# Two quarter-size column groups multiplied by seven products of halves, with their weights summed by accumulating loads and the engines' chains linked half a step apart

## The chip, the cores and the metric

The kernel runs on one core of a Trainium2 chip. Its engines are called here PE (matrix products; PEld is its weight load), DVE (element-wise), ACT (activation functions and casts), POOL and SP (SP issues transfers, POOL can too). The metric is the device time of one launch in microseconds (us). Before the change it is 914.13 us, the median of three runs from 913.93 to 915.59 us.

## The reference, cut to what matters

```python
xn = rms_norm(x, norm_pre_w)                      # x: 256 tokens x 2048
z = xn @ w_in                                     # 2048 x 13312
u, g_lru, q, k, v, g_attn, m_lru, m_attn = split(z)
u = centred_depthwise_conv(u, conv_w, conv_b)     # width 4
h = rg_lru(u, forward) + rg_lru(u, reverse)
y_a = h * silu(g_lru)
y_b = windowed_gqa(rope(q), rope(k), v, sink) * silu(g_attn)
merged = sigmoid(m_lru) * (y_a @ w_proj_a) + sigmoid(m_attn) * (y_b @ w_proj_b)
out = x + rms_norm(merged @ w_out)
```

All is float32. Two of the matrices are touched by the change: the recurrent merge gate (`m_lru`, 2048 columns of `w_in`) and projection pa (`w_proj_a`, 2048 x 2048).

## The kernel before, in words

The weights pass through the core once, in 152 loads of 1 MB. Each load is one *step*. A "quad" step holds 512 rows by 512 columns of a weight matrix, and four quads make one chunk of 512 output columns; a "blk" step holds all 2048 rows of 128 columns. Steps run in the order of `load_plan` (L53): input u, merge gate 0, v, then blocks of the gates gl and ga and of u, with merge-gate chunks 1, 2 and 3 set between (`BETWEEN`), then k, four times (q, pa), four chunks of ma, four of pb, four of o.

Products are made to near float32 accuracy from two parts of each operand: the high part is a cast to float32r and the low part is the rest. A 512-column product takes three matmuls (high by high, high by low, low by high; `mm3`, L155).

Each step is cut into two *half steps*, numbered `hs`. In half step `hs` the program issues, in this order, the loads that have come due (`fetch(i + 3)`, three `raw` buffers), then all work registered for it (`at`, `soon`), then the split of the weights for half step `hs + 4` (`split`, L146: ACT casts `wh`, L115; DVE subtracts to `wl`, L116; five buffers of each), then the matmuls of `hs` itself. The engines each follow this order on their own, so PE can only be held up by a `wh` or `wl` that is late, by a PSUM bank that isn't free, or by an activation part that is late.

In the recurrent stage `lru_pair` (L410) spreads the work of one pair of blocks over 20 half steps: convolution on DVE (`conv`), the gate matmuls `gate..` in four PSUM banks of tag `bg` (which has four), sigmoids, tanh, exp and square root on ACT, products and scans on DVE. Pairs start `PACE` half steps apart. Attention heads start four half steps apart.

SBUF work tiles of 4 KB a partition come from a pool `units` of 32.

Of the kernel before, what the change touches and what calls it, by code (L numbers as in the profile page):

```python
# [20 lines left out]
P = 128  # L21
D = 2048
S = 256
# [5 lines left out]
UNITS = 32  # L29
# [3 lines left out]
LRU0 = 13  # L33
BETWEEN = {1: 1, 3: 2, 5: 3}
XN = 15
PACE = (20,) + (16,) * 6 + (12,) * 2
HEAD0 = 5
FIRST = 8
# [14 lines left out]
def load_plan():  # L53

    plan = []

    def quad(m, c):
        plan.extend(("quad", m, c, i) for i in range(4))

    def pair(m, c, n):  # L60
        plan.extend(("blk", m, c + (n + i) * P, 0) for i in range(2))

    quad("w_in", U0)
    quad("w_in", ML0)
    quad("w_in", V0)
    for i in range(8):
        pair("w_in", GL0, 2 * i)
        pair("w_in", GA0, 2 * i)
        if i < 6:
            pair("w_in", U0, 2 * i + 4)  # L70
        if i in BETWEEN:
            quad("w_in", ML0 + BETWEEN[i] * 512)
    quad("w_in", K0)
    for c in range(4):
        quad("w_in", Q0 + c * 512)
        quad("w_proj_a", c * 512)
    for c in range(4):
        quad("w_in", MA0 + c * 512)
    for c in range(4):
        quad("w_proj_b", c * 512)  # L80
    for c in range(4):
        quad("w_out", c * 512)
    return plan


def body(ctx, tc, x, xT, wall, wlru, pvec, npost, ident_d, mask_d, rope_d, out):
    nc = tc.nc
    const = ctx.enter_context(tc.tile_pool(name="const", bufs=1))
    units = ctx.enter_context(tc.tile_pool(name="units", bufs=UNITS))
    ring = ctx.enter_context(tc.tile_pool(name="ring", bufs=3))  # L90
# [30 lines left out]
    plan = load_plan()  # L121
# [16 lines left out]
    raws, parts = {}, {}  # L138

    def fetch(i):  # L140
        if i >= len(plan) or i in raws:
            return
        raws[i] = ring.tile([P, 2048], F32, tag="raw", name=f"raw{i}", bufs=3)
        nc.sync.dma_start(raws[i], wall[i])

    def split(q, c=0, w=1024, cast=nc.scalar.copy):  # L146
        i, h = q // 2, q % 2
        if i >= len(plan):
            return
# [10 lines left out]
    def add_pair(name, act, done):  # L160
# [23 lines left out]
        for j in range(2):  # L184
            steps.append(("blk", lambda h, wh, wl, j=j: half(j, h, wh, wl)))

    def total(dst, ps):
        t = half_unit("total", "lo", F32, 1)
        nc.scalar.copy(t, ps[:, :, 1])
        nc.vector.tensor_tensor(dst, ps[:, :, 0], t, ALU.add)  # L190

    def add_rows(name, act, done, spare=False, last=False):
# [33 lines left out]
        for g in range(4):  # L226
            steps.append(("quad", lambda h, wh, wl, g=g: half(g, h, wh, wl)))
# [134 lines left out]
    for g in range(4):  # L362
        steps.append(("quad", lambda h, wh, wl, g=g: u_quad(g, h, wh, wl)))
# [3 lines left out]
    def upad_tile(n):  # L367
        t = small.tile([P, 2, S + 3], F32, tag="upad", name=f"upad{n}", bufs=2)
        nc.gpsimd.memset(t[:, :, 0:2], 0.0)
        nc.gpsimd.memset(t[:, :, S + 2:S + 3], 0.0)  # L370
        upads[n] = t
        return t
# [4 lines left out]
    def evac_quad(n):  # L377
        scaled(upad_tile(n)[:, :, 2:2 + S], ups[n // 2][:, :, 0])
# [31 lines left out]
    def lru_pair(n, b):  # L410
# [7 lines left out]
        def weights():  # L418
            v["wh"] = unit(f"lwh{n}", F32R, (P, 1024))
            v["wl"] = unit(f"lwl{n}", F32R, (P, 1024))  # L420
            parts_of(v["wh"], v["wl"], v.pop("raw"))

        def conv(j):
            if j == 0:
                v["u"] = half_unit(f"uu{n}", "uu")
            up = upads[n]
# [3 lines left out]
            nc.vector.tensor_scalar(u, up[:, j, 0:S], cw[:, 0:1], cb, ALU.mult, ALU.add)  # L430
            for tap in range(1, 4):
                nc.vector.scalar_tensor_tensor(u, up[:, j, tap:tap + S], cw[:, tap:tap + 1], u, ALU.mult, ALU.add)  # L432
# [3 lines left out]
        def u_parts():  # L436
            v["uh"] = half_unit(f"uh{n}", "ph", F32R, 1)
            v["ul"] = half_unit(f"ul{n}", "pl", F32R, 1)
            parts_of(v["uh"], v["ul"], v["u"])
# [46 lines left out]
        def y_parts():  # L486
            q = n // 2
            ya[q] = pair_unit(f"ya{q}")
            parts_of(ya[q][:, :, 0], ya[q][:, :, 1], sgl[n // 4][:, n % 4:n % 4 + 2])

# [12 lines left out]
        at(b + 21 + G, y_parts)  # L503

    def silu_evac(units_list, n):
        def done(ps):
# [5 lines left out]
            nc.scalar.activation(sg, dst, AF.Sigmoid)  # L512
            soon(lambda: nc.vector.tensor_tensor(dst, dst, sg, ALU.mult))
        return done

    def u_evac(n):
        return lambda ps: total(upad_tile(n)[:, :, 2:2 + S], ps)

    tm, sm, ms = [], [], []

    def gate_evac(units_list, c, scale=1.0):
        def done(t, ps):
            if t == 0:
                units_list.append(unit(f"mg{c}", F32, (P, 2, 512)))
            nc.scalar.activation(units_list[c][:, t], ps, AF.Sigmoid, scale=rtok[:, t:t + 1] if scale is None else scale)
        return done

    add_rows("ml0_", xs, gate_evac(tm, 0, None), True)
# [9 lines left out]
    add_rows("v_", xs, v_evac)  # L538

    b = LRU0  # L540
    for c in range(8):
        add_pair(f"gl{2 * c}", xn, silu_evac(sgl, 2 * c))
        add_pair(f"ga{2 * c}", xn, silu_evac(sga, 2 * c))
        if c < 6:
            add_pair(f"u{2 * c + 4}", xn, u_evac(2 * c + 4))
        if c in BETWEEN:
            add_rows(f"ml{BETWEEN[c]}_", xn, gate_evac(tm, BETWEEN[c]))
# [295 lines left out]
```

## Time and profile before

| | |
|---|---|
| median of three runs | 914.13 us |
| the profiled execution's own time | 914.31 us |
| its span, first to last instruction | 912.5 us |
| PE busy | 903.0 us (99%), 4638 matmul records |
| PEld busy | 772.1 us (85%) |
| DVE busy | 610.6 us (67%), 841 instructions |
| ACT busy | 551.7 us (60%), 775 instructions |
| moved by transfers | 172.18 MB, mean 189 GB/s |
| mean granted TensorE clock | 0.997 |

A matmul's bar in the trace is longer than its share of PE's time, since matmuls overlap: two that follow each other start closer together than one lasts. PE's pace is therefore read from starts, or from the chain of waits, where each piece is cut at the start of the next. For DVE and ACT the mean duration of a group is close to what one instruction takes.

### The profile page before, as it was taken

To read this page: it belongs to the slowest core of one execution; us is meant where nothing else is said; L and a number is where in the kernel's file an instruction comes from. 1 tells how busy PE (TensorE), PEld (TensorE's weight loads), DVE (VectorE), ACT (ScalarE), POOL (GpSimd) and SP (SyncE) were. 2 spreads that over 40 slices of the span, in tenths; PEclk is the share of its full clock that TensorE was granted. 3 is DMA by queue.
4 is the path that set the end of the run, shared out by engine and by line. 5 is a ranking of instruction groups with operands and counts; after the bars stand their busy time and mean duration, and the time that the engine had idled before them with its cause. 6 is when DMAs were issued, how large, how long until landed. Compare 5 with 4: busy or idle time off the path is not lost.

```text
span 912.5 us, 11845 instructions
## 1 busy us (share of the span) xinstructions
PE 903.0 (99%) x4638; PEld 772.1 (85%) x4638; DVE 610.6 (67%) x841; ACT 551.7 (60%) x775; POOL 1.4 (0%) x23
## 2 busy tenths in 40 slices
PE   9999999999999999999999999999999999999996
PEld 8888888888888888888888888888888888888885
DVE  6897877768676868596755666666654655555554
ACT  7969578685969496949445545454554544444451
POOL 0000000000000000000000000000000000000000
PEclk9999999999999999999999999999999999999998
DMA  9744564545564455536654444444444555558532
GB/s 329 261 180 170 194 254 181 208 142 191 199 216 176 184 180 214 181 136 217 218 190 154 173 166 158 151 172 163 161 167 175 204 191 185 185 191 316 185 139 92
DMA packets 27703, 172.18 MB, mean 189 GB/s; under 512 B 3072, under 2 KB 3968, under 8 KB 8576
## 3 DMA queue, kind: packets, MB, share of 16 engines
q1 hardware_dynamic: 26928, 170.27, 51.7%
q10 hardware_dynamic: 720, 1.16, 0.3%
q8 instruction: 36, 0.59, 0.2%
q14 instruction: 19, 0.16, 0.0%
HBM read 169.32 MB, written 2.10 MB: 188 GB/s over the span
## 4 chain that ended last, share of the span: by engine, by line
PE 98%; DMA 1%; DVE 0%; ACT 0%; issue 0%; SPq 0%; DVEq 0%
PE ga L175 6%; PE gl L175 6%; PE u L175 5%; PE o L156 4%; PE o L158 4%; PE o L157 4%; PE ga L177 3%; PE gl L177 3%; PE u L177 3%; PE u_ps L360 2%; PE gate L156 1%; PE gate L158 1%; PE gate L157 1%; PE ma__6163 L156 1%; PE pa__5483 L156 1%; PE ma__5943 L156 1%
## 5 line engine op out<-in xcount | busy, mean ns | idle before, releaser
L116 DVE TENSOR_TENSOR wl<-raw,wh 128x1024 fp32r<-128x1024 f32 (+1 forms) x306 | 370.5, 1215 | 265.0 <-ACT wh L115 264.1
L115 ACT CAST wh<-raw 128x1024 fp32r<-128x1024 f32 (+1 forms) x305 | 315.5, 1045 | 212.1 <-PE o L158 37.0
L175 PE MATMUL gl<-xn,wh 128*128 128x512 f32 x256 | 62.5, 391 | 0.0
L175 PE MATMUL ga<-xn,wh 128*128 128x512 f32 x256 | 62.5, 391 | 0.0
L175 PEld LDWEIGHTS gl<-xn,wh 128*128 128x128 f32 x256 | 46.8, 188 | 9.0
L175 PEld LDWEIGHTS ga<-xn,wh 128*128 128x128 f32 x256 | 46.8, 188 | 9.0
L156 PE MATMUL o<-wh,ms 128*128 128x512 f32 x128 | 49.9, 390 | 0.0
L158 PE MATMUL o<-wh,ms 128*128 128x512 f32 x128 | 49.8, 389 | 0.0
L157 PE MATMUL o<-wl,ms 128*128 128x512 f32 x128 | 49.8, 389 | 0.0
L175 PE MATMUL u<-xn,wh 128*128 128x512 f32 x192 | 46.8, 391 | 0.0
L175 PEld LDWEIGHTS u<-xn,wh 128*128 128x128 f32 x192 | 35.3, 188 | 6.8
L617 ACT ACTIVATE p<-p,nm 128x256 f32<-128x256 f32 x32 | 16.0, 502 | 36.3 <-DVE nm L615 36.3
L177 PEld LDWEIGHTS gl<-xn,wl 128*128 128x128 f32 x256 | 33.0, 191 | 1.3
L177 PEld LDWEIGHTS ga<-xn,wl 128*128 128x128 f32 x256 | 33.0, 191 | 1.3
L177 PE MATMUL ga<-xn,wl 128*128 128x256 f32 x256 | 33.7, 283 | 0.0
L177 PE MATMUL gl<-xn,wl 128*128 128x256 f32 x256 | 33.7, 283 | 0.0
L158 PEld LDWEIGHTS o<-wh,ms 128*128 128x128 f32 x128 | 24.0, 188 | 5.0
L157 PEld LDWEIGHTS o<-wl,ms 128*128 128x128 f32 x128 | 24.0, 188 | 5.0
L156 PEld LDWEIGHTS o<-wh,ms 128*128 128x128 f32 x128 | 24.0, 188 | 4.9
L177 PEld LDWEIGHTS u<-xn,wl 128*128 128x128 f32 x192 | 24.6, 191 | 0.9
L177 PE MATMUL u<-xn,wl 128*128 128x256 f32 x192 | 24.9, 283 | 0.0
L432 DVE SCALAR_TENSOR_TENSOR uu<-upad,pv,uu 128x256 f32<-128x256 f32 x48 | 23.3, 485 | 2.3
(345 smaller groups left out, 2012.7 us busy)
## 6 DMA issues: line engine op xcount, KB each, us to landing
raw<-wall_dram SPq DMA_DIRECT2D x149, 1024.0 KB, 4.8
lraw<-wlru_dram SPq DMA_DIRECT2D x8, 512.0 KB, 5.7
raw<-wall_dram SPq DMA_DIRECT2D x4, 512.0 KB, 7.0
xr<-x_dram SPq DMA_DIRECT2D x4, 512.0 KB, 10.2
raw<-wall_dram SPq DMA_DIRECT2D x4, 256.0 KB, 5.1
xT<-xT_dram SPq DMA_DIRECT2D x4, 256.0 KB, 6.4
np<-npost_dram SPq DMA_DIRECT2D x2, 512.0 KB, 7.7
out_dram<-yw SPq DMA_DIRECT2D x4, 256.0 KB, 2.1
```

What stands on the lines that cost most here:

```text
L115: cast(h, src)
L116: nc.vector.tensor_tensor(l, src, h.bitcast(F32), ALU.subtract)
L156: nc.tensor.matmul(ps, wh, xh, start=start, stop=False)
L157: nc.tensor.matmul(ps, wh, xl, start=False, stop=False)
L158: nc.tensor.matmul(ps, wl, xh, start=False, stop=stop)
L175: nc.tensor.matmul(ps, wh[:, sl], a, start=k == 0, stop=k == KT - 1)
L177: nc.tensor.matmul(ps[:, 1], wl[:, sl], a[:, 0], start=False, stop=False)
L360: nc.tensor.matmul(ups[b // 2][:, b % 2, 0], w[:, sl], a[:, m], start=k == 0 and n == 0, stop=k == KT - 1 and n == 2)
L432: nc.vector.scalar_tensor_tensor(u, up[:, j, tap:tap + S], cw[:, tap:tap + 1], u, ALU.mult, ALU.add)
L617: nc.scalar.activation(p[:, t], p[:, t], AF.Exp, bias=nm[:, t:t + 1], accum_out=dn[:, t:t + 1])
```

## The change

**Seven products.** Merge-gate chunks 1 and 2, and pa's chunks 2 and 3, are no longer multiplied chunk by chunk. Each pair of chunks is a product of a 256 x 2048 by a 2048 x 1024 matrix; both are cut in halves each way (128 tokens, 1024 rows of the weights, 512 columns), and the four quarter results come from seven products (`add_seven`, `SEVEN`) in place of eight. Each product is two *woven* steps, so fourteen steps with half the matmuls of a plain step (12, against 24) stand where eight plain ones stood. `spread` sets one woven step behind every three plain ones in the recurrent stage, and one behind one or two plain ones among pa and pb. The total is 164 steps.

**Sums on the left.** Four of the seven products take differences of quarters of the activations: `sums` makes them on DVE (L600) from the normalised input (`xe`) and from the recurrent branch's output (`ye`), and splits them into high and low parts.

**Sums on the right.** The weights of q5, n7, n6 and q4 are sums of quarters. The tile of the earlier product is kept (pool `chain`, two buffers), and POOL issues a load that adds the next quarter to it (`accum_op=ALU.add`, L870), once both halves of the tile are split. There are 16 such loads of 1 MB. SP issues 145 loads of 1 MB from the loop, against 149 before.

**Putting together.** `after` copies or combines each product on ACT or DVE; two products that share a PSUM bank accumulate in it, so that bank is held from one woven step to the next. Pool `units` has 31 tiles.

**Links half a step apart.** `ahead` issues the cast `wh` for `hs + 4` in `hs`, and `low` the subtraction `wl` in `hs + 1` (before, both in `hs`). `lag_parts` does the same to other splits, `total` and the silu to theirs; heads get a half step between `expo` and `powers`. The recurrent pairs start an even 18 half steps apart (`LRU_PACE`), the heads three. The convolution reads a tile without borders, so POOL's memsets of borders are gone. ma's chunks stand between the q's, and pa comes behind them.

```diff
+CHAIN = 2
-LRU0 = 13
+LRU0 = 14
+LRU_PACE = 18
-PACE = (20,) + (16,) * 6 + (12,) * 2
+HEADS_PACE = 3
+FILL = ((0,), (1,), (), (2, 3))
...
+SEVEN = {
+    "p1": (0, 0, "r"), "p2": (0, 1, None), "q5": (1, 0, "r"), "n3": (1, 1, "q"),
+    "n7": (1, 0, "q"), "n6": (0, 0, "q"), "q4": (0, 1, "q"),
+}
...
+    def lag_parts(h, l, src):
+        nc.scalar.copy(h, src)
+        soon(lambda: nc.vector.tensor_tensor(l, src, h.bitcast(F32), ALU.subtract))
...
     def fetch(i):
-        if i >= len(plan) or i in raws:
+        if i >= len(steps) or i in raws or i in grown:
             return
-        raws[i] = ring.tile([P, 2048], F32, tag="raw", name=f"raw{i}", bufs=3)
-        nc.sync.dma_start(raws[i], wall[i])
+        if i in grow:
+            raws[i] = chain.tile([P, 2048], F32, tag="c", name=f"chain{i}")
+        else:
+            raws[i] = ring.tile([P, 2048], F32, tag="raw", name=f"raw{i}", bufs=3)
+        nc.sync.dma_start(raws[i], wall[rows_of[steps[i][0]]])
...
+    def add_seven(name, m, cols, left, take):
...
+        def half(op, s, h, wh, wl):
+            fresh = op in ("p1", "q5", "n7", "q4")
+            if fresh and s == 0 and h == 0:
+                ps["at"] = bank(f"{name}{op}", (P, 512))
+            d = ps["at"]
+            for j in range(2):
+                k = 4 * s + 2 * h + j
+                a, b = left(op, k)
+                sl = slice(j * 512, (j + 1) * 512)
+                for n, (x, y) in enumerate(((a, wh), (a, wl), (b, wh))):
+                    nc.tensor.matmul(d, x, y[:, sl], start=fresh and k == 0 and n == 0, stop=k == 7 and n == 2, skip_group_check=not fresh)
+            if s == 1 and h == 1:
+                soon(lambda: after(op, d))
...
+            elif op == "n6":
+                w = t["w"] = scrap(3)
+                tt(w, d, t["p1"], ALU.subtract)
+                tt(t["x"], t["x"], w, ALU.add)
+                tt(t["q5"], t["q5"], w, ALU.add)
+                soon(lambda x=t["x"], y=t["q5"]: [take(0, 1, x), take(1, 1, y)])
...
+        def less(d, a, b):
+            e[d] = e[b] if isinstance(b, str) else eight(unit(f"{name}{d}"))
+            for n in range(2):
+                f = [e[o][:, 4 * n:4 * n + 4] if isinstance(o, str) else fm(*o, n) for o in (a, b)]
+                nc.vector.tensor_tensor(e[d][:, 4 * n:4 * n + 4], *f, ALU.subtract)
...
+    for c in range(8):
+        lru_pair(2 * c, LRU0 + LRU_PACE * c)
+    steps += spread(plain, add_seven("ml", "w_in", [ML0 + 512, ML0 + 1024], lefts(xn, xe), lambda t, j, d: gate_take(tm, 1 + j, t, d)), 8, 3)
...
+    steps += spread(plain, add_seven("pa", "w_proj_a", [3 * 512, 2 * 512], lefts(pa, ye), lambda t, j, d: take_pa(3 - j, t, d)), 2, 1.3)
...
+    def low(q):
+        i, h = q // 2, q % 2
+        wh, wl = parts[q]
+        nc.vector.tensor_tensor(wl, raws[i][:, h * 1024:(h + 1) * 1024], wh.bitcast(F32), ALU.subtract)
+        if h == 1 and i in grow:
+            n = grow[i]
+            raws[n] = raws[i]
+            nc.gpsimd.dma_start(raws[n], wall[rows_of[steps[n][0]]], accum_op=ALU.add)
+
+    def ahead(q):
+        if q < 2 * len(steps):
+            i, h = q // 2, q % 2
+            parts[q] = [ring.tile([P, 1024], F32R, tag=f"w{s}", name=f"w{s}{i}_{h}", bufs=5) for s in "hl"]
+            nc.scalar.copy(parts[q][0], raws[i][:, h * 1024:(h + 1) * 1024])
+            soon(lambda: low(q))
```

How instructions stand on three engines shows the places that the prediction speaks of. In the rows, a name carries the step and half that it belongs to: `wl26_1` is the low part for the second half of step 26, `gr2` belongs to the recurrent pair that starts at block 2.

DVE in the recurrent stage, where the scans of pair 2 meet the convolution of pair 4; before:

```order
L430 TENSOR_SCALAR uu4_1531<-upad4_1180,pv_90 128x256
L432 SCALAR_TENSOR_TENSOR uu4_1531<-upad4_1180,pv_90,uu4_1531 128x256 x3
L116 TENSOR_TENSOR wl26_1_1537<-raw26_1462,wh26_1_1536 128x1024
L499 TENSOR_TENSOR gi2_1326<-gi2_1326,th2_1378 128x1024
L430 TENSOR_SCALAR uu4_1531<-upad4_1180,pv_90 128x256
L432 SCALAR_TENSOR_TENSOR uu4_1531<-upad4_1180,pv_90,uu4_1531 128x256 x3
L116 TENSOR_TENSOR wl27_0_1560<-raw27_1506,wh27_0_1559 128x1024
L476 SCALAR_TENSOR_TENSOR gr2_1325<-a2_1407,gi2_1326 128x256
L477 SCALAR_TENSOR_TENSOR gr2_1325<-a2_1407,gi2_1326 128x256
L476 SCALAR_TENSOR_TENSOR gr2_1325<-a2_1407,gi2_1326 128x256
L477 SCALAR_TENSOR_TENSOR gr2_1325<-a2_1407,gi2_1326 128x256
L116 TENSOR_TENSOR lwl4_1580<-lraw4_1439,lwh4_1579 128x1024
```

and in the change (`xee4l` is the low part of one of the activation sums):

```order
L467 SCALAR_TENSOR_TENSOR gr2_1298<-a2_1366,gi2_1299 128x256
L468 SCALAR_TENSOR_TENSOR gr2_1298<-a2_1366,gi2_1299 128x256
L467 SCALAR_TENSOR_TENSOR gr2_1298<-a2_1366,gi2_1299 128x256
L468 SCALAR_TENSOR_TENSOR gr2_1298<-a2_1366,gi2_1299 128x256
L420 TENSOR_SCALAR up4_1177<-up4_1177,pv_93 128x256
L423 SCALAR_TENSOR_TENSOR up4_1177<-up4_1177,pv_93 128x254
L423 SCALAR_TENSOR_TENSOR up4_1177<-up4_1177,pv_93 128x255 x2
L866 TENSOR_TENSOR wl26_1_1510<-raw26_1440,wh26_1_1509 128x1024
L420 TENSOR_SCALAR up4_1177<-up4_1177,pv_93 128x256
L423 SCALAR_TENSOR_TENSOR up4_1177<-up4_1177,pv_93 128x254
L423 SCALAR_TENSOR_TENSOR up4_1177<-up4_1177,pv_93 128x255 x2
L113 TENSOR_TENSOR xee4l_1521<-xee1_1172,xee4h_1520 128x1024
```

The four scans and one half of the convolution now stand in one half step, where they stood on two sides of a weight split, and a sum's low part has come between the splits.

PE at the second gate group of pair 4 (`gate4_10` and `gate4_11` are the third and fourth PSUM bank that the pair takes); before, the row in which the fourth bank begins had no wait:

```order
L156 MATMUL gate4_10_1716<-uh4_1601,lwh4_1579 128x256
L157 MATMUL gate4_10_1716<-ul4_1602,lwh4_1579 128x256
L158 MATMUL gate4_10_1716<-uh4_1601,lwl4_1580 128x256
L156 MATMUL gate4_11_1723<-uh4_1601,lwh4_1579 128x256
L157 MATMUL gate4_11_1723<-ul4_1602,lwh4_1579 128x256
```

and in the change:

```order
L152 MATMUL gate4_10_1727<-uh4_1609,lwh4_1582 128x256
L153 MATMUL gate4_10_1727<-ul4_1610,lwh4_1582 128x256
L154 MATMUL gate4_10_1727<-uh4_1609,lwl4_1583 128x256
L152 MATMUL gate4_11_1734<-uh4_1609,lwh4_1582 128x256 [waits Activation_49]
L153 MATMUL gate4_11_1734<-ul4_1610,lwh4_1582 128x256
```

The fourth bank now waits for ACT, whose sigmoids empty the first one. The same wait stands at the pairs 4 to 12; at pair 14 it is one on DVE, and pairs 0 and 2 have none.

POOL's queue; before, it held the memsets of borders:

```order
L369 MEMSET upad4_1180 128x2x2 [waits DVE_49,Pool_49]
L370 MEMSET upad4_1180 128x2
L369 MEMSET upad6_1508 128x2x2 [waits DVE_49,Pool_49]
L370 MEMSET upad6_1508 128x2
L369 MEMSET upad8_2027 128x2x2 [waits DVE_49,Pool_49]
```

and in the change it holds the accumulating loads (here pa's):

```order
L870 DMA chain112_5685<-wall_dram 128x2048 [waits DMAHW2_49,DMASW6_49,DVE_49]
L870 DMA chain114_5831<-wall_dram 128x2048 [waits DMAHW4_49,DMASW7_49,DVE_49]
L870 DMA chain125_6317<-wall_dram 128x2048 [waits DMAHW5_49,DMASW0_49,DVE_49]
L870 DMA chain128_6436<-wall_dram 128x2048 [waits DMAHW0_49,DMASW1_49,DVE_49]
L870 DMA chain125_6317<-wall_dram 128x2048 [waits DMASW2_49,DVE_49]
L870 DMA chain128_6436<-wall_dram 128x2048 [waits DMASW3_49,DVE_49]
L870 DMA chain125_6317<-wall_dram 128x2048 [waits DMASW4_49,DVE_49]
L870 DMA chain128_6436<-wall_dram 128x2048 [waits DMASW5_49,DVE_49]
```

Each waits for DVE's last subtraction from the tile and for the load into it before.

More of the change, by code (lines that the diff above doesn't have):

```diff
@@ L28 @@
 EPS = 1e-6
-UNITS = 32
+UNITS = 31
+CHAIN = 2
 DECAY = 12
@@ L182, in half @@
                 soon(lambda: done(got["ps"]))
-        for j in range(2):
-            steps.append(("blk", lambda h, wh, wl, j=j: half(j, h, wh, wl)))
+        return [(("blk", m, c + (n + j) * P, 0), lambda h, wh, wl, j=j: half(j, h, wh, wl), None) for j in range(2)]
     def total(dst, ps):
@@ L536, in v_evac, with spread @@
         nc.vector.scalar_tensor_tensor(vl, ps, rtok[:, t:t + 1], vh.bitcast(F32), ALU.mult, ALU.subtract)
-    add_rows("v_", xs, v_evac)
-    b = LRU0
+    steps += add_rows("v_", "w_in", V0, xs, v_evac)
+    def spread(plain, woven, start, every):
+        plain, at_ = list(plain), [start + int(n * every) for n in range(len(woven))]
+        for n, i in reversed(list(enumerate(at_))):
+            plain.insert(i, woven[n])
+        assert at_[-1] <= len(plain) - len(woven), (at_, len(plain))
+        return plain
@@ new lines, in add_seven, with scrap, after @@
+    def add_seven(name, m, cols, left, take):
+        ps, t = {}, {}
+        def half(op, s, h, wh, wl):
[11 more added lines that the diff above has]
+                soon(lambda: after(op, d))
+        def scrap(n):
+            if n % 2 == 0:
+                t["two"] = unit(f"{name}t{n}", F32, (P, 2, 512))
+            return t["two"][:, n % 2]
+        def after(op, d):
+            tt = nc.vector.tensor_tensor
+            if op == "p1":
+                t["p1"] = scrap(0)
+                nc.scalar.copy(t["p1"], d)
+            elif op == "p2":
+                take(0, 0, d)
+            elif op == "q5":
+                t["q5"] = scrap(1)
+                nc.scalar.copy(t["q5"], d)
+            elif op == "n3":
+                t["x"] = scrap(2)
+                nc.scalar.copy(t["x"], d)
+            elif op == "n7":
+                tt(t["x"], t["x"], d, ALU.subtract)
+            elif op == "n6":
[4 more added lines that the diff above has]
+                soon(lambda x=t["x"], y=t["q5"]: [take(0, 1, x), take(1, 1, y)])
+            else:
+                tt(t["w"], d, t["w"], ALU.subtract)
+                soon(lambda w=t["w"]: take(1, 0, w))
+                t.clear()
+        out = []
+        for op, (c, r, key) in SEVEN.items():
+            for i in range(2):
+                out.append((("quad", m, cols[c], 2 * r + i), lambda h, wh, wl, op=op, i=i: half(op, i, h, wh, wl), key and (name, key, i)))
+        return out
@@ new lines, in lefts, with left @@
+    def lefts(pairs, e):
+        of = {"p1": (0, 0), "p2": (0, 1), "q4": (1, 1), "q5": "e1", "n3": "e4", "n7": "e3", "n6": "e2"}
+        def left(op, k):
+            o = of[op]
+            if isinstance(o, str):
+                return [a[:, k] for a in e[o]]
+            k += 8 * o[1]
+            return [pairs[k // 2][:, k % 2, m, o[0] * P:(o[0] + 1) * P] for m in range(2)]
+        return left
+    xe, xe_when = sums("xe", xt)
+    xe_when([XE + n for n in (0, 6, 12, 18)])
+    plain = []
@@ new lines, in ms_flip, with ms_part, branch, rows @@
+    def ms_flip(c, held):
+        for q in range(2):
+            held[q] = bank(f"ms_ps{c}{q}")
+            for j in range(2):
+                n = 2 * q + j
+                for t in range(2):
+                    nc.tensor.transpose(held[q][:, j, t * P:(t + 1) * P], sm[c][:, t, n * P:(n + 1) * P], ident)
+    def ms_part(c, q, held):
+        a = pair_unit(f"ms{2 * c + q}")
+        ms[2 * c + q] = a
+        lag_parts(a[:, :, 0], a[:, :, 1], held.pop(q))
+    def branch(name, m, y, take):
+        pairs = {}
+        def rows(q):
+            a = pairs[q] = pair_unit(f"{name}y{q}")
+            lag_parts(a[:, :, 0], a[:, :, 1], y[q // 2][:, q % 2 * 2:q % 2 * 2 + 2])
+        def when(hs):
+            for q in range(8):
+                at(hs + q, lambda q=q: rows(q))
+        def chunk(c):
+            return add_rows(f"{name}{c}_", m, c * 512, pairs, lambda t, d: take(c, t, d))
+        return pairs, when, chunk
@@ L769, in body @@
             if hs >= FIRST:
-                split(hs + 4)
+                ahead(hs + 4)
             half(h, *parts.pop(hs))
```

239 lines of the change are left out of this document (110 added, 129 removed).

## The prediction

> **What bounds the kernel now.** I read the page first: its head, the busy times and the chain that ended last.
>
> ```profile
> span 912.5 us, 11845 instructions
> PE 903.0 (99%) x4638; PEld 772.1 (85%) x4638; DVE 610.6 (67%) x841; ACT 551.7 (60%) x775; POOL 1.4 (0%) x23
> PE 98%; DMA 1%; DVE 0%; ACT 0%; issue 0%; SPq 0%; DVEq 0%
> ```
>
> PE is the bound from end to end: 98% of the chain is PE work. A busy PE isn't yet a PE that can't be held up, so next come the waits of PE alone, which name all that ever held it.
>
> ```profile
> PE spin L240 <- POOL eps L235: 1.0, 1, 1.0
> PE u_ps L360 <- ACT wh L115: 0.8, 2, 0.5
> PE kp L583 <- issue: 0.4, 1, 0.4
> ```
>
> That is 2.2 us in all, most of it at the start. Then the chain in order of time gives PE's pace and the tail. A wide matmul (512 columns) takes 3.65/16 = 0.228 us of PE, a half-width one 1.91/16 = 0.119 us.
>
> ```profile
> 79.40 1.91 PE gl L177 x16
> 81.31 3.65 PE gl L175 x16
> ...
> 905.03 0.24 PE o L158
> 905.27 0.02 issue
> 905.29 0.70 ACT junk L733 x2
> ```
>
> So a plain quad step is 24 x 0.228 = 5.47 us, a blk step 3.65 + 1.91 = 5.56 us. After the last matmul, 912.5 - 905.3 = 7.2 us of tail remain, which the change leaves alone. The time can fall only by PE work that goes away, and rises by whatever starves PE.
>
> How near are the two engines that feed PE? The stretches of the recurrent stage (80 to 440 us) and of q, pa, ma (440 to 760 us), with columns PE, PEld, DVE, ACT, POOL busy, clock, transfer share and GB/s:
>
> ```profile
> 80.00:440.00 360.00, 359.56 (x1995) 314.31 (x1995) 265.96 (x320) 268.97 (x361) 0.68 (x10) 1.00 0.53 191
> 440.00:760.00 320.00, 320.00 (x1553) 268.75 (x1552) 197.50 (x335) 159.25 (x241) 0.00 (x0) 1.00 0.48 172
> ```
>
> DVE and ACT are busy 74% and 75% of the first and 62% and 50% of the second. The recurrent stage is the tight one.
>
> **The change, part by part.**
>
> *PE work removed.* Each pair of chunks was 8 steps of 24 wide matmuls, 192; now it is 14 of 12, 168. Two pairs save 48, which is also the difference between the two listings of PE (3200 wide matmuls, now 3152; the narrower ones are unchanged in number). 48 x 0.228 = 10.9 us, all of it on the chain.
>
> *Splits added.* Fourteen woven steps replace eight, so there are 2 x 6 x 2 = 24 more weight splits. The sums of activations add 8 splits of the same size and 16 half-size subtractions; the rest is copying and combining. Counted on the listings, DVE gets 32 instructions of 1024 elements and 34 of 512 more, ACT 32 and 6.
>
> ```profile
> L116 DVE TENSOR_TENSOR wl<-raw,wh 128x1024 fp32r<-128x1024 f32 x302 | 367.8, 1222 | 263.8 <-ACT wh L115 262.9
> L432 DVE SCALAR_TENSOR_TENSOR uu<-upad,pv,uu 128x256 f32<-128x256 f32 x48 | 23.3, 485 | 2.3
> L476 DVE TENSOR_TENSOR_SCAN gr<-a,gi 128x256 f32<-128x256 f32 x16 | 10.8, 674 | 0.0
> L460 DVE TENSOR_TENSOR gi<-gi,uu 128x512 f32<-128x512 f32 x16 | 10.3, 685 | 0.0
> L430 DVE TENSOR_SCALAR uu<-upad,pv 128x256 f32<-128x256 f32 x16 | 6.4, 402 | 0.0
> L115 ACT CAST wh<-raw 128x1024 fp32r<-128x1024 f32 x302 | 313.6, 1049 | 211.0 <-PE o L158 37.0 <-PE pb__6626 L158 13.5 <-PE pb__6940 L158 13.5
> L189 ACT COPY total<-ga 128x512 f32<-128x512 f32 x8 | 4.6, 573 | 1.8 <-PE ga L175 1.8
> ```
>
> DVE: 32 x 1.222 + 34 x 0.685 = 62 us, to about 673 us, 75% of a span near 902. ACT: 32 x 1.049 + 6 x 0.573 = 37 us, to some 589 us, 65%. Both lie beside PE on average; if nothing hid them, DVE's 62 us would be the price. The question is the densest place.
>
> That place is half steps 48 to 55, where the first rows shown of the change stand: scans of pair 2, convolution of pair 4 and two of the activation sums. Its DVE list holds 11 instructions of 1024 elements, 9 of 512, 4 scans, and a convolution of 2 plus 6: 11 x 1.222 + 9 x 0.685 + 4 x 0.674 + 2 x 0.402 + 6 x 0.485 = 26.0 us. PE takes 2 x 6 x 0.228 (the two half steps of a woven step, 6 wide matmuls each) + 6 x 2.78 (halves of blk steps) = 19.4 us. DVE falls 6.6 us behind. Its lead: `wl` of half step q is now issued in q - 3, so two plain half steps, 5.5 us, may pass before PE needs it (before, three). Back to back, DVE is a little faster than its means:
>
> ```profile
> 310.41 2.35 DVE L116 TENSOR_TENSOR wl<-raw,wh 128x1024 fp32r<-128x1024 f32 x2
> ```
>
> 1.175 us apiece, 4% less, which makes the lag 5.6 us. So PE waits between 0 (DVE enters this place ahead, since it can subtract as soon as the cast is there) and about 1.1 us (it enters with none to spare). The same count before gives at most 24.0 us against 23.7, and PE never waited. Four other groups of eight half steps exceed PE, at 64, 120, 136 (recurrent) and 224 (pa): 21.3, 22.7 and 22.0 against 19.4, and 22.2 against 19.3, by 1.9 to 3.3 us, inside the lead. I take 1.5 us for all of them, nearer the lower end, since the lead covers four of the five; ends 0 and 8 us.
>
> *Links half a step apart.* They remove waits of DVE and ACT that cost nothing now: the 263.8 us of DVE idle before `wl` and PE's 2.2 us stand side by side. No gain by themselves; the cost is the half step of lead counted above.
>
> *Fourth gate bank.* One `bg` bank is held by the woven products, so at five pairs PE's second gate group waits for ACT's first two sigmoids.
>
> ```profile
> L456 ACT ACTIVATE gi<-gate,pv 128x256 f32<-128x256 f32 x32 | 15.7, 490 | 0.0
> L467 ACT ACT_TABLE_LOAD x14 | 18.0, 1283 | 0.2
> ```
>
> They take 2 x 0.49 = 1.0 us and come one cast (1.05 us) after the half step begins, while PE has that half step's matmuls (2.74 us) and half of a gate group (0.7 us) to do first: 2.0 against 3.4 us, hidden. Behind the waiting matmul stands all of PE. With the cover gone (a table load of 1.28 us and one more cast late on ACT) it costs about 1 us a pair, 5 us in all. Ends 0 and 5; I take 0, since ACT's list has no other work left over at these half steps.
>
> *Accumulating loads.* No row shows one. The nearest are plain loads of the same 1 MB:
>
> ```profile
> q1 hardware_dynamic: 26928, 170.27, 51.7%
> raw<-wall_dram SPq DMA_DIRECT2D x149, 1024.0 KB, 4.8
> DMA to landing us min/median/max: 4.6/4.8/12.1
> ```
>
> Landing: 4.8 us, at most 12.1. The tightest need is among pa's last products: a load is issued after `low` in half step 2i - 2 and cast in 2n - 4, and from step 135 to 139 six half steps lie between, 13.7 us of PE, less 1.2 for the subtraction: 12.5 us. PE starves only if the load takes 19 us, since the cast runs four half steps ahead. Both ends hide. Behind a waiting POOL instruction stand only other accumulating loads; behind a late chain tile on SP stand the next `raw` loads (the window there is 13.7 us too, against 4.8).
>
> Engine time: 170.27 MB took 51.7% of 912.5 us on 16 engines, so 1.05 MB takes 2.9 us of all. One woven step with 1.3 plain ones is 2.74 + 7.11 = 9.85 us of PE and 1.3 x 2.9 = 3.8 us of plain loads, so an accumulating load may hold the engines 6.1 us before transfers fall behind. Lower end 2.9 us (a plain load). For the upper I take 12.1 us, the longest landing, as if it held every engine. I take a value below 6.1, because adding reads the tile as well as the weights, twice the reading of a plain load, 5.8 us. Cost 0.
>
> The Trainium skill, "Collectives: The Full Stack", section "The bandwidth ceiling: the fold count and why AG ≠ RS ≠ AR", says that an add in the transfer path is slow for its two source reads and not for the add, and halves the rate. No run here shows it yet; by it the sum stays as it is, and a rate lower than half would speak for the second rival.
>
> *Sum.* Profiled execution 914.31 - 10.9 + 1.5 = 904.9 us. Its time is 0.2 us over the median, so I predict **904.7 us**.
>
> **Rivals.**
>
> 1. *Forecast*: PE follows its own work; 0 to 4 us are given back. 903.2 to 907.3 us. Chance 0.78.
> 2. *DVE overrun gives most back.* For it: 6.6 us of overrun against a lead of 5.5, and a lead that shrinks by 1.4 us beside each woven half step. Against: PE's 2.2 us of waits with DVE at 74%. If half of each overrun reaches PE: (6.6 + 1.9 + 3.3 + 2.6 + 2.9) / 2 = 8.7 us, 911.9 us. Chance 0.12.
> 3. *Accumulating loads fill the transfer engines: slower than before.* The place is pa's last six accumulations, steps 130 to 141. At four times a plain load, 11.6 us, each falls 11.6 - 6.1 = 5.5 us behind, 33 us, less a lead of 8.2 us (three half steps): 24.8 us lost, 914.1 - 9.4 + 24.8 = 929.5 us. It decides from (9.4 + 8.2) / 6 + 6.1 = 9.0 us a load. For it: nothing shows such a load. Against: the mean share is near one half and a doubled load still fits. Chance 0.07.
> 4. *The gate banks wait*, 5 us: 909.7 us. Against it, the 1.4 us of slack above. Chance 0.03.
>
> That the change doesn't remove the matmuls is excluded by the listings.
>
> **How the numbers follow.** Low 902.9: all 10.9 us less 0.3 for the spread of runs. High 911.5: rival 4, and most of rival 2; what is left out is rival 3, the top of rival 2 and little else. The forecast's own range is 903.2 to 907.3. A measurement here tells from no change what differs by over 0.2%, 1.8 us. Faster than that: 0.78 + 0.03 + 0.09 of rival 2 = 0.90. Within: 0.03 of rival 2. Slower: rival 3, 0.07.
>
> **What would show it right or wrong.** In the profile after: about 4590 matmul records; PE's chain share still 97% or more; the waits of PE under 4 us, with what there is under `wl` between 150 and 180 us from the start; landings of the accumulating loads under 12 us; the pace still 0.228. It is wrong if PE waits on DVE at many places of the recurrent stage (rival 2), if ACT's casts wait for chain tiles after 690 us (rival 3), if gate matmuls wait on ACT (rival 4), or if wide matmuls start further apart.

## The result, and the profile after

The changed kernel takes **903.99 us** (median of four runs, 903.67 to 904.10), beside 914.15 us for the kernel before on the same chip (913.93 to 915.59). The ratio is 0.9885, with a 95% interval from 0.9868 to 0.9902: faster by 1.15%, 10.2 us. The forecast was 904.7 us, in a range from 902.9 to 911.5.

The page of the changed kernel: head, busy times, the shares of the chain that ended last, and the two load queues (packets, MB, share of 16 engines).

```profile
span 902.2 us, 11861 instructions
PE 892.3 (99%) x4590; PEld 763.9 (85%) x4590; DVE 664.2 (74%) x899; ACT 579.1 (64%) x807; POOL 14.6 (2%) x23
PE 93%; DVE 3%; ACT 2%; DMA 1%; issue 1%; SPq 0%; DVEq 0%
q1 hardware_dynamic: 26352, 166.08, 50.5%
q0 software_dynamic: 2304, 16.78, 10.1%
```

PE did 10.7 us less work and is still busy 99% of the span. What is new is the chain: PE's share fell from 98% to 93%, because for some 45 us the chain runs through DVE and ACT. PE was busy beside them, so this is no loss by itself, but it shows that there PE's work waits on theirs with next to nothing to spare. The waits of PE, all that the view lists:

```profile
PE spin L234 <- POOL eps L229: 1.0, 1, 1.0
PE u_ps L354 <- ACT wh L105: 0.7, 1, 0.7
```

1.7 us, both before the recurrent stage, against 2.2 before. And the chain in order of time around the dense place (start, length, what):

```profile
150.44 0.58 DVE gr L468
151.03 0.32 DVE up L420
...
162.38 1.13 DVE wl L866
163.51 1.21 DVE xee L600 x2
164.71 0.61 DVE ul L113
...
165.37 0.39 PE gate L153
...
165.87 0.12 PE gate L152
...
169.04 0.32 PE gate L152
```

Scans, convolution, subtractions of weights and of the sums stand one behind the other on DVE, until `ul` of pair 4, the third to start, is done at 164.71 + 0.61 = 165.32 us. PE takes it up 0.05 us later. Its matmul there stands for 0.39 us in the chain where its neighbours stand for 0.12, so PE was touched for about 0.27 us. At 169.04 us it was touched once more, for 0.2 us: that is the matmul with which the fourth gate bank of the pair begins, and ACT's sigmoid `gi` had ended 0.05 us before. Both lie at the place the prediction named, and the cover was used up to nearly nothing: from 140 to 172 us (PE, PEld, DVE, ACT, POOL busy, clock, transfer share, GB/s) DVE was busy 31.4 of 32 us. The first row is the kernel before, with 27.4, the second the change.

```profile
140.00:172.00 32.00, 32.00 (x156) 27.00 (x155) 27.36 (x34) 23.08 (x28) 0.14 (x2) 1.00 0.48 169
140.00:172.00 32.00, 31.89 (x183) 27.83 (x182) 31.39 (x41) 22.67 (x29) 0.87 (x1) 1.00 0.57 185
```

Over the longer stretches nothing is that tight:

```profile
80.00:440.00 360.00, 359.89 (x1994) 314.46 (x1993) 293.13 (x348) 273.40 (x367) 7.12 (x8) 1.00 0.64 212
640.00:760.00 120.00, 120.00 (x561) 100.14 (x561) 95.76 (x120) 71.02 (x86) 6.09 (x7) 1.00 0.79 231
```

DVE went from 266.0 to 293.1 us of the recurrent stage's 360. In pa's stretch the transfer engines were busy 79%, the highest share of any of the long stretches, and PE never idled.

The end of the chain shows where the time went:

```profile
81.24 3.65 PE gl L171 x16
...
894.00 0.24 PE o L154
...
897.20 1.33 DVE yw L854 x2
```

The pace is still 3.65/16 = 0.228 us. PE's last matmul ends at 894.24 us instead of 905.27: 11.0 us earlier, all of the 10.9 us of matmuls that went. The span is only 10.3 us shorter, since the tail behind the last matmul grew by 0.7 us, from 912.5 - 905.27 = 7.23 to 902.2 - 894.24 = 7.96 us. It grew at its very end: from DVE's last `yw` to the end of the span are 902.2 - 898.53 = 3.67 us, before 912.5 - 909.54 = 2.96.

### The profile page after: what moved, and what is told of

It reads as the page before. It is cut to its first block, busy times and chain, and to the rows that moved or that the text cites. A ratio compares the mean times of both kernels' runs of the same rounds, so it can differ in the third digit from the quotient of the medians.

```text
span 902.2 us, 11861 instructions
## 1 busy us (share of the span) xinstructions
PE 892.3 (99%) x4590; PEld 763.9 (85%) x4590; DVE 664.2 (74%) x899; ACT 579.1 (64%) x807; POOL 14.6 (2%) x23
## 3 DMA queue, kind: packets, MB, share of 16 engines
q0 software_dynamic: 2304, 16.78, 10.1%
## 4 chain that ended last, share of the span: by engine, by line
PE 93%; DVE 3%; ACT 2%; DMA 1%; issue 1%; SPq 0%; DVEq 0%
PE ga L171 6%; PE gl L171 6%; PE u L171 4%; PE o L154 4%; PE o L152 4%; PE o L153 4%; PE ga L173 3%; PE gl L173 3%; PE u L173 2%; PE u_ps L354 2%; PE paq L548 2%; PE mlq L548 2%; PE pap L548 1%; PE mln L548 1%; PE pan L548 1%; PE gate L153 1%
## 5 line engine op out<-in xcount | busy, mean ns | idle before, releaser
L866 DVE TENSOR_TENSOR wl<-raw,wh 128x1024 fp32r<-128x1024 f32 x268 | 324.7, 1220 | 131.3 <-ACT wh L876 130.8
L876 ACT CAST wh<-raw 128x1024 fp32r<-128x1024 f32 x268 | 278.6, 1050 | 175.0 <-PE o L154 36.8
L876 ACT CAST wh<-chain 128x1024 fp32r<-128x1024 f32 x48 | 50.0, 1052 | 27.9 <-PE pb__6403 L154 5.0
L866 DVE TENSOR_TENSOR wl<-chain,wh 128x1024 fp32r<-128x1024 f32 x48 | 57.8, 1219 | 13.3 <-ACT wh L876 12.9
L870 POOL DMA_DIRECT2D chain<-wall_dram x16 | 14.1, 880 | 734.6 <-DVE wl L866 725.0
```

The lines of the kernel that those rows point to most:

```text
L866: nc.vector.tensor_tensor(wl, raws[i][:, h * 1024:(h + 1) * 1024], wh.bitcast(F32), ALU.subtract)
L870: nc.gpsimd.dma_start(raws[n], wall[rows_of[steps[n][0]]], accum_op=ALU.add)
L876: nc.scalar.copy(parts[q][0], raws[i][:, h * 1024:(h + 1) * 1024])
```

## The experiments

Six kernels do or undo one part, five price one cost or wait by itself. All times stand beside the kernel before on the same chip (914.1 to 914.5 us). The 95% interval of a ratio is 0.001 to 0.002 wide to each side, 1 to 2 us, so the differences of a few us between two of these kernels are read from their medians and hold only roughly. No two of the medians compared below as different have runs that overlap.

### The links without the seven products

Merge gate and pa as before in plain chunks; all else of the change stays.

```diff
-LRU_PACE = 18
+LRU_PACE = 16
...
-    xe_when([XE + n for n in (0, 6, 12, 18)])
...
-        if c == 4:
-            plain += add_rows("ml3_", "w_in", ML0 + 3 * 512, xn, gate_evac(tm, 3))
+        if c in (1, 3, 5):
+            i = (c + 1) // 2
+            plain += add_rows(f"ml{i}_", "w_in", ML0 + i * 512, xn, gate_evac(tm, i))
...
+    steps += plain
```

> Part of the change alone: the links half a step apart, the new order of pa and ma and the convolution without borders, but every chunk as four plain steps (no seven products, no accumulating loads; recurrent pairs 16 half steps apart). Theory (the gain is PE work removed, the links give nothing by themselves because PE waited only 2.2 us before): 914 us, between 913 and 915, with 3200 wide matmuls. Rival (the links give part of the gain): 911 us or less.

Measured: 913.75 us, ratio 0.9992 (0.9982 to 1.0001). The new order and the links alone are worth nothing that can be told from noise: where PE isn't waiting, there is nothing to gain.

### The seven products in the merge gate alone

```diff
-    plain = [st for c in (0, 1) for st in pa_chunk(c)]
+    plain = [st for c in range(4) for st in pa_chunk(c)]
...
-    ye_when([b + n for n in YE])
-    steps += spread(plain, add_seven("pa", "w_proj_a", [3 * 512, 2 * 512], lefts(pa, ye), lambda t, j, d: take_pa(3 - j, t, d)), 2, 1.3)
+    steps += plain
```

> The change with seven products in the recurrent merge gate only; pa's four chunks are plain. Theory (each pair of chunks gives 24 wide matmuls x 0.228 = 5.5 us, the two add up): 903.99 + 5.5 = 909.5 us, and 914.15 - 5.5 = 908.7 from the other side, so between 908.5 and 909.7. Rival (one of the two pairs gives nearly all, the other is eaten by waits): 904 or 914 us.

Measured: 909.86 us, ratio 0.995 (0.9935 to 0.9965). Half of the matmuls, nearly half of the gain: 4.6 us here, and 5.9 us more with the other half. The time is 0.2 us above the range of the theory. The expectation left out the longer end of the program, which this kernel has too (3.8 us behind DVE's last instruction, against 2.96 before). With it the gain counts by matmuls removed, and neither of the two stages eats what the other gains.

### Links undone, all and one kind at a time

First both kinds: a weight's low part `wl`, and the low parts that `lag_parts` makes, are subtracted in the half step of their casts.

```diff
     def lag_parts(h, l, src):
         nc.scalar.copy(h, src)
-        soon(lambda: nc.vector.tensor_tensor(l, src, h.bitcast(F32), ALU.subtract))
+        nc.vector.tensor_tensor(l, src, h.bitcast(F32), ALU.subtract)
...
-            soon(lambda: low(q))
+            low(q)
```

> The change with the subtraction of each split back in the half step of its cast (weights and the other splits); silu, totals and heads stay linked apart. Theory as predicted (the links cost and gain nothing by themselves, half a step of lead more): 904 us within 1. Rival (at DVE's 81% in the recurrent stage its idling behind ACT's casts no longer fits, so the links carry the denser stage): PE waits on DVE there, 906 to 910 us.

Measured: 909.49 us, ratio 0.9951 (0.9935 to 0.9968). The rival was right: in the woven kernel the links carry 5.5 us of the gain. The largest wait of PE, then the same 32 us as above, and the chain that leads to the matmul that waited:

```profile
PE gate L152 <- ACT gi L447: 2.8, 1, 2.8
```

```profile
140.00:172.00 32.00, 29.33 (x168) 25.56 (x166) 30.35 (x39) 20.99 (x27) 0.87 (x1) 1.00 0.55 171
```

```profile
166.65 1.22 DVE xee L600 x2
...
167.89 0.02 ACT xee3h L112
...
169.43 1.89 ACT wh L876 x2
...
171.69 0.38 ACT gi L447
...
172.11 0.39 PE gate L152
```

DVE did 1.0 us less in those 32 us and PE 2.6 us less. The wait of ACT from which the chain comes, here and then with the change (`xee3h` is the cast of one of the activation sums, `xee`):

```profile
ACT xee3h L112 <- DVE xee L600: 4.8, 1, 4.8
```

```profile
ACT xee3h L112 <- DVE xee L600: 3.6, 1, 3.6
```

DVE comes to `xee` at 166.65 us here and at 163.51 with the change, 3.1 us earlier. ACT idles until `xee` is there, so everything behind `xee3h` in its order is late: a copy, two weight casts, and the sigmoid `gi` of pair 4, for whose bank PE's next gate group stood waiting. It is the fourth-bank wait of the prediction's last rival, set off by DVE's lateness and not by ACT's own list.

Why is DVE later? From the start of the span to `xee` it worked 139.3 us here and 137.5 with the change, and idled 27.3 and 26.0 us. So of the 3.1 us, 1.8 are work that now stands ahead of `xee`: without the links one weight subtraction and `ul` come before it, with them behind it. Only 1.3 us are longer idling. At this place, then, the links help mainly by order: they put subtractions that aren't urgent behind what ACT, and through it PE, waits for. That they also let the engines wait less for each other is the smaller part.

From 160 to 200 us the granted clock was 0.96 as well. It shows right behind the wait: PE's next eight wide matmuls last 3.56 us together, where they last 2.00 us with the change, so 1.6 us more. With the 4.0 us of waits more (5.7 in all against 1.7) that is the 5.6 us by which this span is longer.

```profile
160.00:200.00 40.00, 37.22 (x206) 32.41 (x205) 30.67 (x33) 30.93 (x44) 0.00 (x0) 0.96 0.58 210
```

Then each kind by itself. The weights' link alone undone (`low(q)` at once, `lag_parts` as in the change):

> The change with only the weights' subtraction put back into the half step of its cast; the other splits stay linked apart. Theory (the weights' link carries the gain that undoing all splits' links lost, 5.5 us, since each of 328 weight splits makes DVE wait for a cast): 908 to 910 us. Rival (the links of the activations' splits carry it): 904 to 905 us.

Measured: 914.76 us, ratio 1.0006 (0.9996 to 1.0015): all of the gain is gone, worse than with both kinds undone. Neither theory nor rival expected that. `lag_parts` alone undone:

> The change with only the other splits (recurrent weights and inputs, sums, heads, branch outputs) put back into the half step of their cast; the weights' subtraction stays half a step behind. Theory (the weights' link carries the gain): 904 to 905 us. Rival (the other splits' links carry it): 908 to 910 us. If both halves lose about 2 to 3 us, the two links do the work together.

Measured: 907.01 us, ratio 0.9916 (0.9898 to 0.9934), 3.0 us behind the change and between the two theories. So the prices of the two kinds don't add up: 10.8 and 3.0 us apart, 5.5 us together. PE's waits of the kernel with only the weights' link undone:

```profile
PE gate L153 <- DVE ul L113: 3.1, 3, 2.1
PE q2p L674 <- DVE sg L741: 2.1, 1, 2.1
PE q1p L674 <- DVE sg L741: 2.1, 1, 2.1
```

The last two lie in the heads, outside the weave. The chain there:

```profile
510.58 0.59 ACT ph L112
511.17 0.95 ACT wh L876
512.14 1.23 DVE wl L866
513.37 0.34 DVE sg L741
...
513.76 0.66 PE q1p L674 x4
```

DVE's `sg` stands behind a `wl` that waits for its cast, that stands behind another cast, `ph`, on ACT. To test whether this is what the mixture costs, the heads' low parts were made at once too:

```diff
-            lag_parts(v["h"][:, 2 * q:2 * q + 2], v["l"][:, 2 * q:2 * q + 2], v[q])
+            parts_of(v["h"][:, 2 * q:2 * q + 2], v["l"][:, 2 * q:2 * q + 2], v[q])
...
-            lag_parts(v["h"], v["l"], v.pop("pt"))
+            parts_of(v["h"], v["l"], v.pop("pt"))
...
-            soon(lambda: low(q))
+            low(q)
```

> The weights' low part and the low parts of the attention heads (keys, queries, probabilities) are subtracted in the same half step as their casts; the recurrent pairs, the sums and the projections' inputs stay half a step apart. Undoing the weights' link alone cost 10.8 us, undoing both kinds of link only 5.5 us. Theory: the weave pays some 5.5 us in both, and the other 5 us arise in the heads, where the weights' link is undone and the heads' is not: PE waited 2.1 us twice there, at 514 us and behind 540 us, for the heads' output product on DVE, which stands in DVE's order behind a weight subtraction that itself waits for its cast. With the heads' link undone too these waits go, and the time is 909 to 910.5 us. Rival: it is the recurrent pairs' links against the weights' that cost: 913.5 to 915 us, and the waits of PE in the heads are as before.

Measured: 910.87 us (909.7 to 911.02), ratio 0.996 (0.9946 to 0.9974), 0.4 us above the top of the theory's 909 to 910.5 and far below the rival's. The waits in the heads fall to 0.3 us each, the one under `ul` in the weave is the same to the digit:

```profile
PE gate L153 <- DVE ul L113: 3.1, 3, 2.1
PE q2p L674 <- DVE pl L106: 0.3, 1, 0.3
PE q1p L674 <- DVE pl L106: 0.3, 1, 0.3
```

So of the 10.8 us some 4 arise in the heads (914.76 - 910.87), by a mixture of chains that are half a step apart and chains that are not. Of the rest, the waits of this profiled execution (909.7 us, the fastest of the five) put 3.6 us in the recurrent stage (`ul`, and 0.5 under a `gl`), and 1.4 us ahead of it (`u_ps`, 2.1 us against 0.7 with the change); what the other four executions had more wasn't profiled.

The traces also show what the mixture does in the heads. `sg` isn't later behind `ph`: it ends 3.1 us after `ph` begins with only the weights' link undone, and 3.7 us after it in the last kernel. What changes is which instruction frees the PSUM bank that PE's `q1p` takes next. With the heads' link kept, DVE makes `pl` behind `sg`, at 514.62 us, and PE waits for `sg`. With it undone too, `pl` comes at 509.67 us, ahead of `sg`, and PE waits only for `pl`.

### One half step of lead less

The subtraction `wl` two half steps behind its cast, so that one plain half step less may pass before PE needs it.

```diff
-            soon(lambda: low(q))
+            soon(lambda: low(q), 2)
```

> The change with the weights' subtraction two half steps behind the cast: DVE's lead over PE falls from two half steps (5.5 us) to one (2.7 us). Theory of the dense place (DVE 5.6 us behind at half steps 48 to 55, 1.9 to 3.3 us at four others): 5.6 - 2.7 = 2.9 us at the first, 0 to 0.6 at the others, so about 907.5 us, with PE waits on DVE between 145 and 170 us. Rival (DVE is never really behind, the count overstates it): 904 us.

Measured: 908.52 us, ratio 0.9939 (0.9924 to 0.9954), 4.5 us behind the change and 1.0 us more than the theory's 907.5. PE now waits under `wl`, which is what the prediction's overrun should look like:

```profile
PE v__649 L153 <- DVE wl L866: 1.3, 2, 0.7
PE u L173 <- DVE wl L866: 1.2, 1, 1.2
PE gl L173 <- DVE wl L866: 1.1, 1, 1.1
```

The third of these, at 158 us, is the dense place. It paid 1.1 us where the estimate was 2.9: the count of DVE's lag there is too high by about 1.8 us, or DVE enters the place with about that much to spare. The two can't be told apart by this run. The other two are 1.2 us at 346 us, where at most 0.6 was expected, and 1.3 us in `v` at 56 and 65 us, ahead of the places of the theory. So the total came near the estimate by luck: less than expected at the first place, more elsewhere.

### A denser weave

The prediction's second rival (DVE overruns its lead at several places) priced by making the weave of the merge gate denser: a woven step behind every two plain ones.

```diff
-... lambda t, j, d: gate_take(tm, 1 + j, t, d)), 8, 3)
+... lambda t, j, d: gate_take(tm, 1 + j, t, d)), 16, 2)
```

> One woven step of the merge gate behind every two plain ones (from the sixteenth on) in place of every three: the 28 woven steps lie in 84 steps instead of 112. From 80 to 200 us DVE was busy 102 of 120 us with the change, 85%, so some 16.4 us in four steps of 19.3 us of PE; with one plain step less (4.1 us of DVE, 5.56 of PE) it is 12.3 in 13.8 us, 89%. Theory (DVE's mean decides, the lead covers what is uneven): PE waits under 3 us, 904 to 907 us. Rival (the second of the prediction: uneven places overrun the lead and PE gives back half of each overrun): PE waits 5 to 10 us under subtractions of weights, 909 to 914 us. The accumulating loads come a quarter denser too; in the recurrent stage they have 13.8 us of PE against 2 x 2.9 + 5.7 = 11.5 us of transfer engines, so both theories let them be hidden.

(The 28, 84 and 112 of this expectation count half steps; the woven steps are fourteen.)

Measured: 904.74 us (904.56 to 905.55), ratio 0.9896 (0.9881 to 0.9911). The one new wait of PE of more than 1 us:

```profile
PE mlq L548 <- DVE wl L866: 1.2, 1, 1.2
```

Even a third more of woven work in the same time costs only 0.75 us by the medians. That speaks against the second rival for this stage: while the mean leaves room and the links hold, a lead of two half steps smooths what is uneven.

### The accumulating load

First without the adding: POOL's sixteen loads replace the tile. (The sums of weights are left out, so the products of q5, n7, n6 and q4 are of other numbers; the instructions and bytes read from memory are the same.)

```diff
-            nc.gpsimd.dma_start(raws[n], wall[rows_of[steps[n][0]]], accum_op=ALU.add)
+            nc.gpsimd.dma_start(raws[n], wall[rows_of[steps[n][0]]])
```

> The change with POOL's 16 loads as plain loads that replace the tile and add nothing (left out: the sums of weight quarters, so the products are of other matrices). Theory (the adding is hidden: landing 8.1 us against 12.5 us of room, 5.7 us of engines against 6.1): same time as the change, 904.0 within 0.7; landing near 5 to 6 us and engine share of the software queue near 5% instead of 10.1%. Rival (adding costs PE something somewhere): 1 us or more faster.

Measured: 904.0 us, ratio 0.9889 (0.9871 to 0.9907), the time of the change. The queue and the landing (count, KB, median us), here, and the landing with the change (its queue is shown above):

```profile
q0 software_dynamic: 2304, 16.78, 5.1%
chain<-wall_dram POOLq DMA_DIRECT2D x16, 1024.0 KB, 5.0
```

```profile
chain<-wall_dram POOLq DMA_DIRECT2D x16, 1024.0 KB, 8.1
```

10.1% of 902.2 us is 5.7 us of all sixteen engines for each accumulating load; 5.1% of 901.6 us is 2.9 us for a plain one. Adding doubled the engine time of the same bytes and put 3.1 us on the landing, and all of it was hidden. The doubling agrees with the Trainium skill, "Collectives: The Full Stack", section "The bandwidth ceiling: the fold count and why AG ≠ RS ≠ AR", which says it of an add in a collective's transfer path, for its two source reads; that the second read is the reason is not shown by a run here, only the factor of two.

Then the same cost doubled: each accumulating load twice (so a quarter is added twice, and the sums are of other numbers).

```diff
             nc.gpsimd.dma_start(raws[n], wall[rows_of[steps[n][0]]], accum_op=ALU.add)
+            nc.gpsimd.dma_start(raws[n], wall[rows_of[steps[n][0]]], accum_op=ALU.add)
```

> The change with each accumulating load issued twice, one behind the other (left out: correct sums, a quarter is added twice). Price per step 11.4 us of the transfer engines, landing 16.2 us. Theory of the prediction's third rival (it decides from 9.0 us a load): each of pa's last six accumulations falls 11.4 - 6.1 = 5.3 us behind, 32 us, less 8.2 us of lead: 904 + 24 = 928 us, with ACT waiting for chain tiles after 690 us. Other reading (only landing counts: 16.2 us against 19 us until PE starves): 904 us.

Measured: 936.04 us (935.37 to 936.71), ratio 1.0237 (1.0215 to 1.0259). The mechanism of the third rival exists: past some price per accumulation the kernel becomes slower than before, and PE's new single waits of over 1 us are all at pa's products. Its longest waits of PE and ACT:

```profile
PE pan L548 <- ACT wh L877: 12.4, 2, 6.9
```

```profile
ACT wh L877 <- DMA chain<-wall_dram: 62.1, 6, 13.6
```

The size was missed by 8 us, since engine time wasn't what decided. The engines were held 18.5% of 934.6 us for 32 loads, 5.4 us each, 10.8 a pair. But the second load of a pair can only start once the first has landed, and the chain shows how far apart the first loads of successive pairs were:

```profile
710.50 0.89 POOL chain L870
...
727.71 0.89 POOL chain L870
...
776.02 0.91 POOL chain L870
...
791.22 8.32 DMA chain<-wall_dram
```

These are the first, the second and the fifth of five pairs, and the last landing. From 710.5 to 799.5 us are 89.0 us for five pairs, 17.8 us each, against 9.85 us of PE: 5 x 8.0 = 40 us, less the lead of 8.2, gives 32 us, and 32.0 was measured. That sum was made after the run and fits one case; it says that what bounded an accumulation here is the whole round, from one load's issue to the next one's, and not the engines' share alone. By the same sum (an estimate from these rows) a round begins to cost PE at 9.85 + 8.2 / 5 = 11.5 us, and takes back the change's 10.2 us at 13.5. With single loads a round holds one landing, in pa 7.9 to 9.0 us.

### The longer end

The kernel before with one small load from POOL's queue, which it otherwise doesn't use.

```diff
+    spare = const.tile([P, 64], F32, name="spare")
+    at(60, lambda: nc.gpsimd.dma_start(spare, pvec[:, 0:64]))
```

> The kernel before with one added load of 256 bytes a partition, issued by POOL at half step 60, into a tile that nothing reads. With the change the stretch from DVE's last instruction to the end of the span was 3.67 us, before 2.96 us. Theory: it is the first use of POOL's own load queue that lengthens the end, so the stretch is 3.5 to 3.8 us here and the span some 0.7 us longer than before. Rival: it comes with the number of such loads or with the changed program, and the stretch stays at 2.9 to 3.1 us.

Measured: 915.24 us in one run, span 913.5 us, and DVE's last instruction ends 3.07 us before it (`yw` to 910.43). The theory falls: one use of that queue doesn't lengthen the end by 0.7 us. What the runs do show is where the long end occurs: 3.7 to 3.9 us in each of the ten kernels with eight or more such loads, 2.9 to 3.1 us in the three with none or one (one of these three has the links of the change). The event waits that SP does behind the last line of the kernel go with it, twelve with the change and eight with one load:

```profile
L967 SPq EVENT_SEMAPHORE  x12: 17/28/28, 898.3 to 902.2; - x12
```

```profile
L840 SPq EVENT_SEMAPHORE  x8: 17/28/28, 910.2 to 913.4; - x8
```

That the number of such loads makes these waits is likely, but wasn't tried.

## Why the prediction was right

**PE work removed, 10.9 us: right**, to 0.1 us. PE's end moved by 11.0 us at an unchanged pace, and half of the products gave nearly half of the gain.

**Splits added: counted too high, without a price.** DVE rose by 53.6 us where 62 was counted (26 more instructions of 512 elements in the trace, not 34), ACT by 27.4 where 37 was (six table loads fewer, 38 against 44). Neither entered the sum.

**Give-back at the dense place, 1.5 us: right place, too large, wrong instruction.** PE was touched at 165.4 us, inside the 150 to 180 us that were named, for about 0.27 us, and it was `ul` of the recurrent pair and not `wl` that came last. The step that failed is the count of lag against lead: DVE's list was summed right in kind (DVE busy 98% there), but either the list or the starting point was about 1.8 us too pessimistic, as the run with less lead shows. The other four groups gave back nothing that the waits show.

**Links half a step apart, "no gain by themselves": true as written, wrong as used.** Alone they are worth nothing (913.75 against 914.47 us). But the sum counted only what they cost, half a step of lead, and not what the woven kernel would lose without them: 5.5 us with both kinds undone. The prediction looked at the waits of DVE that they remove, which "cost nothing now", and not at the order that they make: where DVE is busy 98%, what stands ahead of the urgent instruction in its list delays ACT and then PE. The order is shown at one place, 1.8 of 3.1 us at `xee`; for the rest of the 5.5 us it is argued. Had the links been left out of the change, the forecast by the same steps would have been too good by about 5 us.

**Fourth gate bank, 0 us: right with the links**, but not with the 1.4 us of slack that the prediction gave it. At pair 4 the slack was gone and PE lost 0.2 us, since ACT had waited there for `xee` and then had a copy and two weight casts to do before the sigmoids; "no other work left over" was wrong there. Without the links it was the largest single wait, 2.8 us at one pair, where the prediction had put 1 us a pair.

**Accumulating loads, 0 us: right, and the price too**: 5.8 us of engines estimated, 5.7 measured; landings of 7.9 to 9.0 us at pa against a room of 12.5. One landing in the recurrent stage, of the load at 119.5 us, took 12.3 us, just over the 12 that were named. The third rival's point of decision, 9.0 us of engine time a load, is far from 5.7; with the loads doubled the rival came true, but its price was set by rounds of landing, not by engine time alone. (Where the prediction says that a rate lower than half would speak for the second rival, the third is meant.)

**A tail "left alone": wrong by 0.7 us.** It is the one loss that no step of the prediction had, and with the give-back that didn't come it makes the sum: 914.3 - 11.0 + 0.7 = 904.0 us for the profiled execution. That the forecast of 904.7 us came within 0.7 us is in part luck: about 1 us too much of give-back, and 0.5 us less of listed waits of PE (1.7 against 2.2), stood against 0.7 us of tail that was missing.

**Signs.** The number of matmul records, the pace and the waits of PE came as named. PE's share of the chain did not: 93%, where 97% or more was to show the prediction right.

**Rivals.** The second (DVE overrun, 911.9 us) is ruled out by the changed kernel's waits: PE waits nowhere on DVE for as long as the view lists. The denser weave, which pays 0.75 us, agrees. The third and the fourth exist as mechanisms; in the change the third costs nothing and the fourth 0.2 us.

## What to carry to other kernels

Where one engine is 98% of the chain, as here, the gain of leaving out its work can be counted from its pace (10.9 counted, 11.0 measured); the work goes into finding the place where the helpers are fullest and reading how much lead is left there. An order that links engines half a step apart was worth nothing while the helpers had spare time and 5 us once one of them was full, so judge it in the kernel that will need it, and undo or add it as a whole: taking back one kind of link out of two cost up to twice what taking back both did (10.8 against 5.5 us). When such a run loses, follow the chain to the instruction that was late and compare what stood ahead of it, before putting the loss down to waiting. A load that adds cost twice the transfer time of a plain one here and landed some 3 us later; it was free with one landing in a round and cost 32 us with two, so compare the whole round, to the landing, with the time between two uses of the tile.

## What was not expected of the hardware

- An accumulating load of 1 MB held the transfer engines about twice as long as a plain one from the same queue, 5.7 against 2.9 us, and landed in 8.1 against 5.0 us (medians).
- The end of the program behind the last DVE instruction took 0.7 us longer in the kernels with eight or more loads from POOL's queue, and not with one.
- Where PE idled for lack of weights its clock went down too. With the loads doubled (the stretches of the starved products):

```profile
720.00:760.00 40.00, 33.34 (x141) 26.39 (x141) 20.63 (x21) 14.53 (x17) 3.54 (x4) 0.91 0.88 223
760.00:800.00 40.00, 27.82 (x99) 20.56 (x97) 15.55 (x18) 8.62 (x10) 4.41 (x5) 0.79 0.87 202
```

The clock fell to 0.91 and 0.79 while PE was busy 33 and 28 of 40 us. Here the loads set the time anyway. A single wait came with it too, but not always. Behind a wait of 2.05 us (weights' link undone) wide matmuls started 0.43 us apart for 2.6 us, and the clock over the 40 us around was 0.96, as it was behind the 2.8 us with both kinds of link undone. Behind a wait of 2.06 us at the same matmul (the heads' link undone too) the pace stayed at 0.23 us and the clock at 1.00, each in the one execution that was profiled.
